# Two-head sweeps of an mLSTM encoder layer in a fixed order of steps

## The chip, the cores and the metric

The kernel runs on one core of a Trainium2 chip. The metric is the time of one execution on the device in microseconds (us). The core has five engines that each run a queue of their own: PE (matrix products), DVE (vector), ACT (scalar engine), POOL (GpSimd) and SP, which here only issues DMA transfers.

## The reference

One layer on two sequences, of 1024 and 256 rows with 1024 columns each, in float32. A conditioning vector gives a shift, a scale and a gate. The normalized rows go through one wide input projection, whose columns feed a gated convolution branch and a bidirectional mLSTM branch with four heads of width 256. Both branches are projected, merged with gates, projected once more and normalized:

```python
mod = c @ w_ada + b_ada
shift, scale, gate = split(mod, 3)
h = rms_norm(x, norm_g) * (1 + scale) + shift
cb, cc, cx, cz, q, k, v, o, mz, gpre, gmerge = split(h @ w_in)
y_conv = cb * dwconv3(cc * cx) * silu(cz)
hm = mlstm(q, k, v, i, f) + flip(mlstm(flip(q), flip(k), flip(v), ...))
y_m = sigmoid(o) * rms_norm_per_head(hm) * silu(mz)
merged = g_conv * (y_conv @ w_proj_conv) + g_mlstm * (y_m @ w_proj_mlstm)
out = rms_norm(x + gate * (merged @ w_out), final_norm_g)
```

The mLSTM runs in chunks of 128 rows, eight for the first sequence and two for the second, in each direction: a query against the state C, the chunk's own scores, and an update of C.

```python
S = (qc @ kc.T) * Dexp
num = S @ vc + inter_w * (qc @ C)
den = max(abs(sum(S) + inter_w * (qc @ n)), exp(-m_t))
h = num / den
C_new = decay * C + (w * kc).T @ vc
```

## The kernel before

A product of two float32 matrices is made as three products of rounded halves: a high part H, which ACT casts, and a low part L, which is the difference to it, taken by POOL or DVE. Four stages follow one another. First come the normalization and the shift and scale. Then comes the input projection in blocks of 1024 × 640, by Strassen's scheme (`run`); beside it, as generators that take one step per projection block, run the gate's part of the conditioning product (`thirds`) and the decay weights (`weights`). The third stage is the mLSTM with the convolution's projection as filler. The last stage merges, projects and normalizes.

Up to the end of the input projection the engines run their instructions in the order in which the program is written (a manual schedule, the context `hand`, closed before the third stage). From there on a scheduler of the language orders each engine's instructions by its own priorities and by when it expects them to be ready.

In the third stage a backward sweep of a head goes through its ten chunks and stores each query's result in `qcb`. A forward sweep goes the other way and makes the output. The sweep of a chunk consists of these parts, whose tiles the profile names:

- `prep`: ACT makes `vH`, DVE `vL`, the two parts of the weighted values; the parts `kH`, `kL` of the keys are loaded.
- `query`: ACT and POOL split the query into `qH` and `qL`; six products `pq` with the parts `CH`, `CL` of the state (`C0H`, `C0L` forward, `C1H`, `C1L` backward in the old kernel); ACT scales the result into `qcf` (forward) or `qcb` (backward).
- `state`: six products `pu`; DVE updates `C`; ACT casts its high part, POOL takes the low part.
- scores: products of `qT` and `kT`; DVE multiplies them with the decay weights `abc` and sums them into `den`; for two chunks at a time DVE makes `r`, the reciprocal of the denominator.
- tail: ACT and DVE form `Pt` from both directions, PE turns it, ACT copies it to `Ps`, PE multiplies it with the values, DVE adds the queries' results (`sums` below), and ACT sums the squares.
- output: the norm over the row's squares (six small operations of DVE and a root on ACT), ACT scales the rows, PE transposes them, DVE multiplies with the gate `og`, and a DMA stores to `ym_dr`.

The sums are written into the value tile `vN`, and the output is made for blocks of 640, 384 and 256 rows (`mlstm_out`). The filler `zc_units` makes 32 units of 24 products of 320 columns (`acc`), which a hand-written table FILL places among the steps of the forward sweeps. The backward sweep of the next head begins with step 5 of a forward sweep of 18 steps.

Of the kernel before, what the change touches and what calls it, by code (L numbers as in the profile page):

```python
# [41 lines left out]
def encoder_kernel(  # L42
# [776 lines left out]
    def thirds(pool):  # L819

        def total(acc, n):
            pg = misc_tile()
            PE.matmul(pg[0:1, 0:2 * P], ones[:, 0:1], acc[:].rearrange("p s n -> p (s n)"), start=True, stop=True)
            yield
            V.tensor_scalar(out=acc[0:1].rearrange("p s n -> p (s n)"), in0=pg[0:1, 0:2 * P], scalar1=0.5, scalar2=None,
                            op0=ALU.mult)
            for s in range(2):
                store(gb_dr[s:s + 1, n * P:(n + 1) * P], acc[0:1, s])

        late = iter(())  # L830
        for n in range(KT):
            ns = slice(2 * D + n * P, 2 * D + (n + 1) * P)
            acc = pool.tile([P, 2, P], F32, tag="acc", bufs=2, name="gacc")
            G.memset(acc[:], 0.0)
            for s in range(2):
                dma(acc[0:1, s], b_ada[0:1, ns])
            for k in range(0, KT, 4):
                raw = pool.tile([P, 4, P], F32, tag="wg", bufs=1, name="wg")
                dma(raw[:], wada[:, k:k + 4, ns])
                next(late, None)  # L840
                yield
                next(late, None)
                yield
                for i in range(4):
                    for s in range(2):
                        V.scalar_tensor_tensor(out=acc[:, s], in0=raw[:, i], scalar=cols[:, 8 * s + k + i:8 * s + k + i + 1],
                                               in1=acc[:, s], op0=ALU.mult, op1=ALU.add)
            late = chain([None], total(acc, n))
        for _ in late:
            yield  # L850
# [203 lines left out]
    hand.close()  # L1054

# [25 lines left out]
    for i in range(2):  # L1081
        G.memset(vNs[i][:, :, HD:HD + 1], 1.0)
        G.memset(vNs[i][:, :, HD + 1:HD + 2], 0.0)

# [3 lines left out]
    def load_head(h, what):  # L1088
        i, hs = h % 2, slice(h * HD, (h + 1) * HD)
        for t0, tn in ((640, 384), (0, 640), (1024, 256)):  # L1090
            ts_ = slice(t0, t0 + tn)
            cs = slice(t0 // P, (t0 + tn) // P)
            if "k" in what:
                dma(kTs[i][:, :, ts_], kT_dr[hs, ts_].rearrange("(b p) t -> p b t", p=P))
            if "v" in what:
                dma(vNs[i][:, cs, 0:HD], v_dr[ts_, hs].rearrange("(c p) d -> p c d", p=P))
            if "q" in what:
                dma(qTs[i][:, :, ts_], qT_dr[hs, ts_].rearrange("(b p) t -> p b t", p=P))

    vp = mstack.enter_context(tc.tile_pool(name="vp", bufs=2))  # L1100
    mp_ = mstack.enter_context(tc.tile_pool(name="ml", bufs=2))

    def split(pool, src, tag, shape, bufs=2, leng=V):
        H = pool.tile(shape, F32R, tag=tag + "H", bufs=bufs, name=tag + "H")
        L = pool.tile(shape, F32R, tag=tag + "L", bufs=bufs, name=tag + "L")
        A.copy(H[:], src)
        leng.tensor_tensor(out=L[:], in0=src, in1=fp(H[:]), op=ALU.subtract)  # L1107
        return H, L

    class Sweep:  # L1110


        def __init__(self, h, d):
            self.h, self.d = h, d
            self.kT, self.vN, self.qT = (x[h % 2] for x in (kTs, vNs, qTs))
            if d:
                self.todo = [c for c0, n in SEQS for c in range(c0 + n - 1, c0, -1)]
            else:
                self.todo = [c for c0, n in SEQS for c in range(c0, c0 + n - 1)]
            self.ahead = [self.prep(self.todo.pop(0))]  # L1120

        def prep(self, c):
            kH, kL = (mp_.tile([P, HD], F32R, tag="k" + part, bufs=4, name="k" + part) for part in "HL")
            for t, src in zip((kH, kL), kn_dr):
                dma(fp(t[:]), src[c * P:(c + 1) * P, self.h * HD:(self.h + 1) * HD])
            wcol = gcol[:, 3, self.d, self.h, c:c + 1]
            wvH, wvL = (mp_.tile([P, HD + 2], F32R, tag="v" + part, bufs=3, name="v" + part) for part in "HL")
            A.activation(wvH[:], self.vN[:, c, :], AF.Copy, bias=0.0, scale=wcol)
            V.scalar_tensor_tensor(out=wvL[:], in0=self.vN[:, c, :], scalar=wcol, in1=fp(wvH[:]), op0=ALU.mult,
                                   op1=ALU.subtract)  # L1130
            return kH, kL, wvH, wvL

        def query(self, c, dst):
            tsl = slice(c * P, (c + 1) * P)
            pq = psM.tile([P, 512], F32, tag="qc", bufs=1, name="pq")
            qH, qL = split(mp_, self.qT[:, :, tsl], "q", [P, 2, P], leng=G)
            CH, CL = self.parts
            for n, (q, C) in enumerate(((qH, CH), (qL, CH), (qH, CL))):
                for kd in range(2):
                    PE.matmul(pq[:, 0:HD + 2], q[:, kd, :], C[:, kd, :], start=n + kd == 0, stop=n + kd == 3)  # L1140
            A.activation(dst, pq[:, 0:HD + 2], AF.Copy, bias=0.0, scale=gcol[:, 1, self.d, self.h, c:c + 1])

        def state(self, c, first):
            kH, kL, wvH, wvL = self.ahead.pop(0)
            if self.todo:
                self.ahead.append(self.prep(self.todo.pop(0)))
            pu = psM.tile([P, 2, 512], F32, tag="u", bufs=1, name="pu")
# [5 lines left out]
            C = Cbuf[self.d]  # L1153
            if first:
# [4 lines left out]
            self.parts = split(mp_, C[:], f"C{self.d}", [P, 2, HD + 2], bufs=1, leng=G)  # L1159

    def backward(h):
        sw = Sweep(h, 1)
        for (c0, n) in SEQS:
            for c in range(c0 + n - 1, c0 - 1, -1):
                if c < c0 + n - 1:
                    sw.query(c, qcbs[h % 2][:, slot(c), :])
                if c > c0:
                    sw.state(c, c == c0 + n - 1)
                yield

    def forward(h):

        vN, kT, qT, qcb, ssqm = (x[h % 2] for x in (vNs, kTs, qTs, qcbs, ssqms))
        sw = Sweep(h, 0)

        def chunk_pair(c0, n, g):

            abc = abcs.pop(0)
            den = mp_.tile([P, 2, 2], F32, tag="den", name="den")
            r = mp_.tile([P, 2, 2], F32, tag="r", name="r")  # L1180
            qcf = mp_.tile([P, 2, HD + 2], F32, tag="qcf", name="qcf")
            for j in range(2):
                c = g + j
                tsl = slice(c * P, (c + 1) * P)
                if c > c0:
                    sw.query(c, qcf[:, j, :])
                if c < c0 + n - 1:
                    sw.state(c, c == c0)
                yield
                pS = misc_tile()  # L1190
                for kd in range(2):
                    PE.matmul(pS[:, 0:P], qT[:, kd, tsl], kT[:, kd, tsl], start=kd == 0, stop=kd == 1)
                inter = (qcf[:, j, HD:HD + 1] if c > c0 else 0.0,
                         qcb[:, slot(c), HD:HD + 1] if c < c0 + n - 1 else 0.0)
                for d in range(2):
                    V.tensor_tensor_reduce(out=abc[:, d, j, :], in0=pS[:, 0:P], in1=abc[:, d, j, :], op0=ALU.mult,
                                           op1=ALU.add, scale=KSC, scalar=inter[d], accum_out=den[:, j, d:d + 1])

            V.scalar_tensor_tensor(out=r[:], in0=den[:], scalar=-1.0, in1=gcol[:, 2, :, h, g:g + 2].rearrange("p d j -> p j d"),
                                   op0=ALU.mult, op1=ALU.max)  # L1200
            V.tensor_tensor(out=r[:], in0=r[:], in1=den[:], op=ALU.max)
            V.reciprocal(r[:], r[:])
            yield

            Ps = [None, None]

            def tail1(j):
                Pt = mp_.tile([P, P], F32, tag="Pt", name="Pt")
                A.activation(Pt[:], abc[:, 0, j, :], AF.Copy, bias=0.0, scale=r[:, j, 0:1])
                V.scalar_tensor_tensor(out=Pt[:], in0=abc[:, 1, j, :], scalar=r[:, j, 1:2], in1=Pt[:],  # L1210
# [21 lines left out]
            def both():  # L1232
                tail1(1)
                tail2(0)
# [102 lines left out]
    def drain(it):  # L1337
        for _ in it:
            pass
# [193 lines left out]
```

## Time and profile before

| | us |
|---|---|
| median of 3 runs | 1823.41 |
| lowest and highest run | 1821.04 and 1828.21 |
| profiled execution | 1823.46 |
| its span, first to last instruction | 1821.7 |

| engine | busy us | share of the span |
|---|---|---|
| PE | 1693.2 | 93% |
| DVE | 1030.8 | 57% |
| POOL | 831.4 | 46% |
| ACT | 667.6 | 37% |

A row of a view by groups gives the line, the engine, the operation, the tiles and shapes and the count, then the busy time in us and the mean of one in ns, then the engine's idle time just before and what ended it. A row of the waits gives who waited for whom, the total in us, the times and the longest. A row of the chain of waits or of the timeline starts with the start and the duration in us. Products are pipelined, so the pace of PE is the distance of their starts and not the duration of one.

### The profile page before, as it was taken

Reading aid. Unit: us, or ns where it says so; the run is one execution under the profiler, and the core shown is the slowest. Engines: PE = TensorE matmul, PEld = TensorE weight load, DVE = VectorE, ACT = ScalarE, POOL = GpSimd, SP = SyncE. Lnnn points to the kernel's source line nnn. Section 1 sums busy time; section 2 is a strip of 40 time slices with the busy share of each in tenths; the row PEclk is TensorE's granted clock in tenths of the full one; section 3 lists DMA queues with packets and bytes.
Section 4 is the critical chain, followed back from the end, with each engine's and each line's share of the span. In section 5 each row is a group of like instructions: output and inputs, shape, how many; then the busy total and the mean of one; then the engine's idle time right before and its main releaser. Section 6 shows DMA issues by size and latency. Waiting matters only on the chain.

```text
span 1821.7 us, 30022 instructions
## 1 busy us (share of the span) xinstructions
PE 1693.2 (93%) x11438; PEld 1630.9 (90%) x11438; DVE 1030.8 (57%) x1739; ACT 667.6 (37%) x1359; POOL 831.4 (46%) x661
## 2 busy tenths in 40 slices
PE   5789999999899999999999999996888788899997
PEld 1689999999788999999999999996877678799997
DVE  6874333277987554555555333332588777456645
ACT  6552333223434222222222223122576565434323
POOL 3443333234545466666665433333566364232422
PEclk9889999999999999999999999998999999999999
DMA  8223234223655222222221534349767865674631
GB/s 308 63 87 108 98 104 133 84 85 92 168 146 145 62 64 76 76 76 72 68 69 46 167 96 145 121 135 318 256 205 225 282 184 163 217 244 152 225 128 70
DMA packets 231427, 253.28 MB, mean 139 GB/s; under 512 B 13700, under 2 KB 190068, under 8 KB 230260
## 3 DMA queue, kind: packets, MB, share of 16 engines
q1 hardware_dynamic: 231284, 251.37, 43.7%
q8 instruction: 90, 1.47, 0.3%
q14 instruction: 53, 0.43, 0.1%
HBM read 177.85 MB, written 73.47 MB: 138 GB/s over the span
## 4 chain that ended last, share of the span: by engine, by line
PE 54%; DVE 6%; POOL 3%; issue 2%; DMA 2%; ACT 2%; SPq 0%; DVEq 0%; POOLq 0%; ACTq 0%
PE accx L337 35%; PE accd L1312 2%; PE accd L1313 2%; PE accd L1314 2%; PE accd L1423 2%; PE accd L1424 2%; PE accd L1422 2%; PE pq L1140 1%; POOL C1L L1107 1%; PE acc L1313 1%; PE acc L1312 1%; PE acc L1314 1%; POOL wl L161 1%; POOL C0L L1107 1%; PE misc L627 1%
## 5 line engine op out<-in xcount | busy, mean ns | idle before, releaser
L409 DVE TENSOR_TENSOR q<-accx,q 128x640 f32<-128x640 f32 x288 | 233.3, 820 | 420.2 <-PE accx L337 368.0
L161 POOL TENSOR_TENSOR wl<-comb,wh 128x512 fp32r<-128x512 f32 x176 | 236.3, 1344 | 488.3 <-ACT wh L160 403.3
L161 POOL TENSOR_TENSOR wl<-raw,wh 128x512 fp32r<-128x512 f32 x196 | 270.8, 1386 | 194.2 <-ACT wh L160 179.1
L337 PE MATMUL accx<-half,wh 128*128 128x320 f32 x1408 | 268.2, 313 | 5.4 <-ACT wh L160 5.4
L160 ACT CAST wh<-comb 128x512 fp32r<-128x512 f32 x176 | 108.6, 620 | 388.7 <-DVE comb L379 305.7
L337 PEld LDWEIGHTS accx<-half,wh 128*128 128x128 f32 x1408 | 223.5, 190 | 6.8 <-ACT wh L160 5.6
L160 ACT CAST wh<-raw 128x512 fp32r<-128x512 f32 (+1 forms) x212 | 136.2, 648 | 92.5 <-PE accd L1313 27.9
L337 PE MATMUL accx<-half,wl 128*128 128x320 f32 x704 | 162.2, 312 | 0.8 <-POOL wl L161 0.8
L498 ACT ACTIVATE q<-q,zero 128x640 f32<-128x640 f32 x80 | 66.4, 830 | 174.4 <-DVE q L409 155.3
L337 PEld LDWEIGHTS accx<-half,wl 128*128 128x128 f32 x704 | 119.0, 190 | 1.5 <-POOL wl L161 1.5
L1423 PE MATMUL accd<-wl,mH 128*128 128x256 f32 x320 | 90.2, 282 | 0.1
L1422 PE MATMUL accd<-wh,mH 128*128 128x256 f32 x320 | 90.1, 282 | 0.0
L1424 PE MATMUL accd<-wh,mL 128*128 128x256 f32 x320 | 90.0, 282 | 0.0
L337 PE MATMUL accx<-b10H,wh 128*128 128x320 f32 x352 | 82.4, 315 | 6.1 <-ACT q L934 5.9
L337 PE MATMUL accx<-t2H,wl 128*128 128x320 f32 x352 | 81.9, 314 | 4.2 <-POOL wl L161 4.1
L337 PE MATMUL accx<-b00H,wh 128*128 128x320 f32 x352 | 81.8, 314 | 2.4 <-DVE half L248 2.3
L337 PE MATMUL accx<-t2H,wh 128*128 128x320 f32 x352 | 82.4, 316 | 1.8 <-ACT wh L160 1.7
L1312 PE MATMUL acc<-y,wh 128*128 128x320 f32 x256 | 81.8, 323 | 0.7 <-ACT wh L160 0.3
L1313 PE MATMUL acc<-y,wh 128*128 128x320 f32 x256 | 81.2, 317 | 1.1 <-DMA y<-yc_drL 1.1
L337 PE MATMUL accx<-t3H,wh 128*128 128x320 f32 x352 | 80.6, 310 | 1.1 <-ACT wh L160 1.1
L1312 PE MATMUL accd<-y,wh 128*128 128x320 f32 x256 | 78.1, 313 | 3.5 <-DVE og L1283 3.5
L337 PE MATMUL accx<-b10H,wl 128*128 128x320 f32 x352 | 81.1, 312 | 0.2 <-POOL wl L161 0.2
(304 smaller groups left out, 4539.5 us busy)
## 6 DMA issues: line engine op xcount, KB each, us to landing
raw<-in_w_in_dram SPq DMA_DIRECT2D x96, 256.0 KB
raw<-in_w_in_dram SPq DMA_DIRECT2D x44, 512.0 KB
th_dr<-q SPq DMA_DIRECT2D x32, 320.0 KB
th<-th_dr SPq DMA_DIRECT2D x32, 320.0 KB
wa<-in_w_ada_dram SPq DMA_DIRECT2D x8, 1024.0 KB
raw<-in_w_proj_conv_dram SPq DMA_DIRECT2D x16, 512.0 KB
kH<-kn_drH SPq DMA_DIRECT2D x64, 128.0 KB
kL<-kn_drL SPq DMA_DIRECT2D x64, 128.0 KB
```

Source lines behind the costliest of these rows:

```text
L160: A.copy(wh[:], src)
L161: eng.tensor_tensor(out=wl[:], in0=src, in1=fp(wh[:]), op=ALU.subtract)
L337: PE.matmul(acc[:, q, 0:TQ], st_[:, k, :], m_[:, q * TQ:(q + 1) * TQ], start=k == 0 and n == 0, stop=k == 3 and n == 2)
L409: V.tensor_tensor(out=two(dst), in0=ps, in1=two(t), op=ALU.add)
L498: A.activation(out, in_, AF.Tanh, bias=zero[:, 0:1], scale=0.5)
L1107: leng.tensor_tensor(out=L[:], in0=src, in1=fp(H[:]), op=ALU.subtract)
L1312: PE.matmul(accs[q][:, :TQ], wh, yH, start=kt == 0, stop=False)
L1313: PE.matmul(accs[q][:, :TQ], wh, yL, start=False, stop=False)
L1314: PE.matmul(accs[q][:, :TQ], wl, yH, start=False, stop=kt == KT - 1)
L1422: PE.matmul(pd, sH, ws[0][:, k, :], start=kt == 0, stop=False)
L1423: PE.matmul(pd, sH, ws[1][:, k, :], start=False, stop=False)
L1424: PE.matmul(pd, sL, ws[0][:, k, :], start=False, stop=kt == KT - 1)
```

## The change

The manual schedule stays open through the third stage, so each engine runs the order in which that stage is now written. The stage becomes a loop of 56 steps. In step s the forward sweep handles one chunk (`F`), the backward sweep of the next head another (`B_`), the tail of the chunk before (`T1`) is merged and turned, and the one two before (`T2`) is multiplied with the values. Every second step makes the norm of the pair that began four steps earlier, and the two halves of its output stand in that step and in the next.

Steps 0 to 9 hold the first backward sweep with two halves of filler each, 10 to 49 the forward sweeps of the four heads, with a backward sweep in 11 to 40, and 50 to 55 the tails. A half is 12 of a unit's 24 products; the table HALVES says how many a step gets. The sums are written into `qcf` instead of the value tile, and the norm is made for two chunks at a time, 20 times in all instead of 12. Stores are issued at the start of the step after the one that makes them. In `thirds` the same operations are placed by a table of steps, the gate sum (`total`) one step later and its row another step later.

```diff
-    hand.close()
-
     sstack.close()
...
+        def keep_row(n):
+            V.tensor_scalar(out=accs[n][0:1].rearrange("p s n -> p (s n)"), in0=sums[n][0:1, 0:2 * P], scalar1=0.5,
+                            scalar2=None, op0=ALU.mult)
...
         for n in range(KT):
...
+            for t, order, f in ((0, 3, (begin, n)), (0, 2, (load, n, 0)), (1, 0, (bias, n)), (2, 0, (use, n, 0)),
+                                (2, 1, (load, n, 1)), (4, 0, (use, n, 1)), (6, 1, (total, n)), (7, 0, (keep_row, n))):
+                plan.setdefault(4 * n + t, []).append((order, f))
...
+        def sums(self, c):
+            g, j = c - c % 2, c % 2
+            first, last = self.ends(c)
+            r, hm, src = self.r[g], self.qcf[g][:, j, :HD], self.pv[:, :HD]
+            if not first:
+                V.scalar_tensor_tensor(out=hm, in0=hm, scalar=r[:, j, 0:1], in1=src, op0=ALU.mult, op1=ALU.add)
+                src = hm
...
+            A.activation(junk[:], hm, AF.Square, bias=zero[:, 0:1], scale=1.0, accum_out=ssqms[self.i][:, c:c + 1])
...
+        def norm(self, g):
+            sv, rv = ssqms[self.i][:, g:g + 2], rstms[self.i][:, g:g + 2]
+            V.tensor_scalar(out=sv, in0=sv, scalar1=1.0 / HD, scalar2=EPS, op0=ALU.mult, op1=ALU.add)
+            rsqrt_newton(mp_, rv, sv, 2)
             for j in range(2):
+                hm = self.qcf[g][:, j, :HD]
+                A.activation(hm, hm, AF.Copy, bias=0.0, scale=rv[:, j:j + 1])
...
+    HALVES = (2,) * 11 + (1, 0, 1, 1, 0, 1, 0, 1, 0) + (1, 1, 1, 1, 1, 0, 0, 0, 0, 1) + (1, 0, 1, 0, 1, 0, 1, 0, 1, 0) + (2,) * 16
+    END = FIRST + 10 * NH
+    for s in range(END + 6):
...
+        if F:
+            h, c = F
+            fw[h].query(c, pr[h].inter)
+            fw[h].state(c)
+            fw[h].carry(c)
+            pr[h].score(c)
+            pr[h].weigh(c)
+        nxt = at_bw.get(s + 1)
+        if HALVES[s] > 1 or (HALVES[s] and not B_):
+            fills.half()
+            fills.after()
+        if T2:
+            pr[T2[0]].values(T2[1])
+            pr[T2[0]].sums(T2[1])
+        nf = chunk_at(s + 1)
+        if nf:
+            fw[nf[0]].prep(nf[1])
+        if B_:
+            h, i = B_
+            bw[h].query(i, lambda c, h=h: qcbs[h % 2][:, slot(c), :])
+            bw[h].state(i)
+        if T1:
+            pr[T1[0]].merge(T1[1])
+        if B_:
+            bw[B_[0]].carry(B_[1])
+        if T1:
+            pr[T1[0]].turn(T1[1])
+        if HALVES[s]:
+            fills.half()
+            fills.after()
+        if nxt:
+            bw[nxt[0]].prep(nxt[1])
+        for lag, f in ((4, 0), (5, 1)):
+            G_ = chunk_at(s - lag)
+            if G_ and G_[1] % 2 == 0:
+                if f == 0:
+                    pr[G_[0]].norm(G_[1])
+                pr[G_[0]].result(G_[1], f)
...
+    hand.close()
+    ym0.append(load_y(ym_dr, 0))
     mstack.close()
     bstack.close()
```

What the change moves is seen best at three places in the middle of the third stage. The first is ACT's queue, between two results of a forward query (`qcf<-pq`). Before, in a forward sweep beside a backward one:

```order
L1141 ACTIVATE qcf<-pq,gcol 128x258
L1106 CAST qH<-qT_12157 128x256
L1215 COPY Ps<-misc 128x128
L1128 ACTIVATE vH<-vN_12156,gcol 128x258
L1106 CAST C0H<-C_12146 128x516
L1141 ACTIVATE qcb_12144<-pq,gcol 128x258
L1106 CAST qH<-qT_12154 128x256
L1128 ACTIVATE vH<-vN_12156,gcol 128x258
L1230 ACTIVATE qcf,ssqm_12149<-vN_12153,zero 128x256
L1106 CAST C1H<-C_12147 128x516
```

Now, one whole step with both sweeps (`C_12145` is the forward state, `C_12146` the backward one):

```order
L1158 ACTIVATE qcf<-pq,gcol 128x258
L1183 CAST CH<-C_12145 128x516
L1262 ACTIVATE junk,ssqm_12148<-qcf,zero 128x256
L1137 CAST qH<-qT_12153 128x256
L1143 ACTIVATE vH<-vN_12152,gcol 128x258
L1158 ACTIVATE qcb_12143<-pq,gcol 128x258
L1237 ACTIVATE Pt<-abc,r 128x128
L1183 CAST CH<-C_12146 128x516
L1245 COPY Ps<-misc 128x128
L1137 CAST qH<-qT_12156 128x256
L1143 ACTIVATE vH<-vN_12155,gcol 128x258
```

The squares (`junk,ssqm`) now stand ahead of both casts for the next forward chunk and of Pt, and the backward state's cast ahead of Ps and of both casts for the next backward chunk.

The second place is DVE's queue around a norm (`ssqm` to `rstm`). Before, in the norm of five chunks:

```order
L1270 TENSOR_SCALAR ssqm_12149<-ssqm_12149 128x5
L501 SCALAR_TENSOR_TENSOR th<-th,acc 128x320
L1129 SCALAR_TENSOR_TENSOR vL<-vN_12156,gcol,vH 128x258
L138 RECIPROCAL rs_r<-rs_r 128x5
L139 TENSOR_TENSOR rs_t<-rs_r 128x5
L140 TENSOR_TENSOR rs_t<-rs_t,ssqm_12149 128x5
L141 TENSOR_SCALAR rs_t<-rs_t 128x5
L1157 SCALAR_TENSOR_TENSOR C_12147<-C_12147,decay,pu 128x516
L142 TENSOR_TENSOR rstm_12151<-rs_t,rs_r 128x5
L1129 SCALAR_TENSOR_TENSOR vL<-vN_12156,gcol,vH 128x258
L1155 COPY C_12146<-pu 128x516
```

Now, from the second half of Pt to the result:

```order
L1238 SCALAR_TENSOR_TENSOR Pt<-abc,r,Pt 128x128
L1180 SCALAR_TENSOR_TENSOR C_12146<-C_12146,decay,pu 128x516
L1144 SCALAR_TENSOR_TENSOR vL<-vN_12155,gcol,vH 128x258
L1270 TENSOR_SCALAR ssqm_12148<-ssqm_12148 128x2
L138 RECIPROCAL rs_r<-rs_r 128x2
L139 TENSOR_TENSOR rs_t<-rs_r 128x2
L140 TENSOR_TENSOR rs_t<-rs_t,ssqm_12148 128x2
L141 TENSOR_SCALAR rs_t<-rs_t 128x2
L142 TENSOR_TENSOR rstm_12150<-rs_t,rs_r 128x2
L1281 SCALAR_TENSOR_TENSOR og<-misc,mhq,og 128x256
```

Other work that stood between the first operation and the reciprocal, and between the last two, has gone from there, and the result that needs the norm follows it at once.

The third place is PE's queue around the transposes for an output. Before:

```order
L1312 MATMUL acc<-y,wh 128x320
L1282 MATMUL misc<-ident,vN_12156 128x128
L1192 MATMUL misc<-kT_12152,qT_12154 128x128 x2
L1282 MATMUL misc<-ident,vN_12156 128x128 x3
L1150 MATMUL pu<-vH,kH 128x258
L1140 MATMUL pq<-C0H,qH 128x258 x2
L1140 MATMUL pq<-C0H,qL 128x258
```

Now, from the end of a half of the filler over the transposes (`ident,qcf`) to the next step's query and state:

```order
L1362 MATMUL acc<-y,wl 128x320
L1279 MATMUL misc<-ident,qcf 128x128 x2
L1157 MATMUL pq<-CH,qH 128x258 x2
L1157 MATMUL pq<-CH,qL 128x258 x2
L1157 MATMUL pq<-CL,qH 128x258 x2
L1168 MATMUL pu<-vH,kH 128x258
L1169 MATMUL pu<-vH,kL 128x258
L1170 MATMUL pu<-vL,kH 128x258
```

Single products of several units stood beside one another before; now each group is whole, and the next step's query and state follow the transposes.

More of the change, by code (lines that the diff above doesn't have):

```diff
@@ L831, in thirds @@
-        for n in range(KT):
[L832 to L848, printed above, removed]
@@ L849, in thirds, with begin, bias, load @@
-        for _ in late:
+        plan, accs, raws, sums = {}, {}, {}, {}
+        def begin(n):
+            accs[n] = pool.tile([P, 2, P], F32, tag="acc", bufs=2, name="gacc")
+            G.memset(accs[n][:], 0.0)
+        def bias(n):
+            for s in range(2):
+                dma(accs[n][0:1, s], b_ada[0:1, 2 * D + n * P:2 * D + (n + 1) * P])
+        def load(n, j):
+            raws[n] = pool.tile([P, 4, P], F32, tag="wg", bufs=1, name="wg")
+            dma(raws[n][:], wada[:, 4 * j:4 * j + 4, 2 * D + n * P:2 * D + (n + 1) * P])
@@ new lines, in use, with total @@
+        def use(n, j):
+            for i in range(4):
+                for s in range(2):
+                    k = 8 * s + 4 * j + i
+                    V.scalar_tensor_tensor(out=accs[n][:, s], in0=raws[n][:, i], scalar=cols[:, k:k + 1],
+                                           in1=accs[n][:, s], op0=ALU.mult, op1=ALU.add)
+        def total(n):
+            sums[n] = misc_tile()
+            PE.matmul(sums[n][0:1, 0:2 * P], ones[:, 0:1], accs[n][:].rearrange("p s n -> p (s n)"), start=True, stop=True)
@@ L850, in thirds @@
+        for t in range(max(plan) + 1):
+            for _, f in sorted(plan.get(t, ()), key=lambda x: x[0]):
+                f[0](*f[1:])
             yield
@@ L1114, in __init__ @@
             self.h, self.d = h, d
[L1115 to L1131, printed above, removed]
@@ L1133, in query @@
-        def query(self, c, dst):
-            tsl = slice(c * P, (c + 1) * P)
+            self.vN, self.qT = vNs[h % 2], qTs[h % 2]
+            self.order, self.first, self.has_state, self.has_query = [], set(), set(), set()
+            for c0, n in SEQS:
+                cs = list(range(c0, c0 + n))
+                if d:
+                    cs.reverse()
+                self.order += cs
+                self.has_state.update(cs[:-1])
+                self.has_query.update(cs[1:])
+                self.first.add(cs[0])
@@ L1378, in encoder_kernel, with chunk_at, plan @@
-    drain(fill)
-    drain(out)
+    FIRST = 10
+    fills = Filler()
+    fills.load_w(0)
+    load_v(0, 5, 8)
+    fw, bw, pr = {}, {}, {}
+    at_bw = {}
+    for h in range(NH):
+        bw[h], fw[h], pr[h] = Sweep(h, 1), Sweep(h, 0), Pairs(h)
+        for i in range(NC):
+            at_bw[10 * h + i + (h > 0)] = (h, i)
+    def chunk_at(s):
+        h, c = divmod(s - FIRST, NC)
+        return (h, c) if 0 <= h < NH else None
+    todo3 = {}
+    def plan(s, f, *args):
+        todo3.setdefault(s, []).append((f, args))
@@ new lines, in encoder_kernel @@
+    for h in range(NH):
+        s0 = FIRST + 10 * h
+        if h:
+            b0 = 10 * h + 1
+            free = FIRST + 10 * (h - 2)
+            for c0, c1, last in ((5, 8, 7), (0, 5, 4), (8, 10, 9)):
+                plan(max(2, free + last + 1), load_piece, h, c0, c1)
+                plan(max(2, free + last + 2), load_v, h, c0, c1)
+        else:
+            for c0, c1 in ((0, 5), (8, 10)):
+                plan(0, load_piece, h, c0, c1)
+                plan(0, load_v, h, c0, c1)
+        for g in range(0, NC, 2):
+            plan(s0 + g - 2, pr[h].load, g)
+            plan(s0 + g + 2, pr[h].load_og, g)
```

401 lines of the change are left out of this document (203 added, 198 removed).

## The prediction

> **What bounds the kernel now.** I read the busy time by stretches first. The change rewrites the stage between the last product of the input projection and the first product of the merge; its two stretches are 1244–1301 us (first backward sweep) and 1301–1582 us (four forward sweeps with the other backward sweeps among them).
>
> ```profile
> core 0: us, PE busy (x) PEld busy (x) DVE busy (x) ACT busy (x) POOL busy (x), PEclk, DMA share, GB/s
> 1244.00:1301.00 57.00, 49.67 (x319) 47.69 (x320) 16.85 (x30) 20.42 (x43) 26.94 (x24) 0.92 0.91 312
> 1301.00:1582.00 281.00, 237.74 (x1579) 212.94 (x1577) 212.57 (x556) 174.72 (x456) 148.27 (x135) 0.98 0.66 207
> ```
>
> PE is busy 85% of the second stretch, DVE 76%, ACT 62%: no engine is full, and each waits for the others. The stretch holds 40 forward chunks, so 281/40 = 7.0 us for each. The waits of the stage, and then of the projection stage, show where PE itself stands:
>
> ```profile
> PEld pq L1140 <- POOL C1L L1107: 17.9, 25, 2.0
> ...
> PE misc L1192 <- DMA qT<-qT_dr: 11.5, 1, 11.5
> ```
>
> ```profile
> PE misc L823 <- DVE gacc L846: 9.0, 7, 3.6
> ```
>
> The first is 25 short waits (0.7 us) for a state's low part, the second the stage's first load. The third is the gate sum in the projection stage. The chain of waits gives the pace of PE where it waits for nothing, and the merge's start:
>
> ```profile
> 1199.91 6.74 PE accx L337 x46
> ...
> 1267.70 0.73 PE pq L1140 x6
> 1269.25 0.76 DVE C L1157
> 1270.03 0.64 ACT C1H L1106
> ...
> 1582.32 0.63 PE accd L1312
> ```
>
> So 0.147 us for a filler product, 0.122 us for a sweep product. A half unit (12 products) is 1.76 us; a query and a state (12) are 1.46 us. From the end of a state on DVE to its cast on ACT go 0.02 us.
>
> **The change part by part.** *The gate sum.* Its product moves one step, so some 48 projection products (7.0 us), further behind its inputs. The longest of the seven waits was 3.6 us: all 9.0 us go. DVE has the same instructions; the two biases and the row's store move one step too, on SP, where nothing waits for them. I take −9 us, between −12 and 0 (0 if weights become late instead).
>
> *Steps 0 to 9, the first backward sweep.* Each step has two halves, a query and a state: 3.52 + 1.46 = 5.0 us on PE. The 5.2 MB of conv halves now stand ahead of the pieces of keys and queries on SP; at the 312 GB/s above they take 17 us, so the first steps run behind the loads. Ten steps end near 1304 us, within 1299 to 1312; before, the first forward query ran at 1301 (the second stretch is cut there), with 16 halves done where the new order has 20. This part costs 3 us.
>
> *Steps 10 to 49.* Here the whole sum lies. The engines run their rows in order, and the order rows show that in each two-head step ACT and DVE wait for each other twice. DVE: forward state, weights, sums; then ACT: squares, query cast, value cast, backward query's result, first half of Pt; then DVE: second half of Pt, backward state; then ACT: state cast, turned Pt, casts for the next backward step; then DVE: value rest, result, and only then the next forward state. The rows that price them (count and mean of the whole stage):
>
> ```profile
> L1129 DVE SCALAR_TENSOR_TENSOR vL<-vN,gcol,vH 128x258 fp32r<-128x258 f32 x64 | 44.2, 693 | 6.6 <-ACT vH L1128 6.6
> L1157 DVE SCALAR_TENSOR_TENSOR C<-C,decay,pu 128x516 f32<-128x516 f32 x48 | 35.8, 747 | 24.4 <-PE pu L1152 15.8 <-POOL C0L L1107 3.7 <-PE misc L1213 2.0
> L1210 DVE SCALAR_TENSOR_TENSOR Pt<-abc,r,Pt 128x128 f32<-128x128 f32 x40 | 19.4, 498 | 6.4 <-ACT Pt L1209 6.3
> L1228 DVE SCALAR_TENSOR_TENSOR vN<-qcb,r,vN 128x256 f32<-128x256 f32 x24 | 17.8, 744 | 0.4
> ...
> L1224 DVE SCALAR_TENSOR_TENSOR vN<-qcf,r,misc 128x256 f32<-128x256 f32 x32 | 15.3, 477 | 7.1 <-PE misc L1220 7.1
> L1196 DVE CUSTOM_DVE_ANT_0 abc<-misc,abc,qcf 128x128 f32<-128x128 f32 x32 | 11.1, 347 | 10.3 <-PE misc L1192 7.2 <-ACT qcf L1141 2.9
> L1196 DVE CUSTOM_DVE_ANT_0 abc<-misc,abc,qcb 128x128 f32<-128x128 f32 x32 | 11.0, 345 | 0.7 <-ACT qcb L1141 0.7
> L1155 DVE COPY C<-pu 128x516 f32<-128x516 f32 x16 | 10.9, 682 | 11.9 <-PE pu L1152 11.7
> L1199 DVE SCALAR_TENSOR_TENSOR r<-den,gcol 128x4 f32<-128x4 f32 x20 | 10.6, 528 | 0.1
> ...
> L1283 DVE SCALAR_TENSOR_TENSOR og<-misc,mhq,og 128x256 f32<-128x256 f32 x16 | 7.5, 479 | 5.6 <-DMA og<-og_dr 3.4 <-PE misc L1282 1.4 <-PE acc L1313 0.7
> L1201 DVE TENSOR_TENSOR r<-r,den 128x4 f32<-128x4 f32 x20 | 7.3, 365 | 0.1
> ...
> L1196 DVE CUSTOM_DVE_ANT_0 abc<-misc,abc 128x128 f32<-128x128 f32 x16 | 4.6, 286 | 3.3 <-PE misc L1192 3.3
> ...
> L1228 DVE SCALAR_TENSOR_TENSOR vN<-qcb,r,misc 128x256 f32<-128x256 f32 x8 | 3.8, 481 | 3.3 <-PE misc L1220 3.3
> ...
> L1202 DVE RECIPROCAL r<-r 128x4 f32<-128x4 f32 x20 | 3.4, 169 | 0.2
> ```
>
> ```profile
> L1128 ACT ACTIVATE vH<-vN,gcol 128x258 fp32r<-128x258 f32 x64 | 32.3, 510 | 26.4 <-PE pu L1151 19.7 <-DMA qT_dr<-q 4.7 <-DMA vN<-v_dr 1.5
> L1106 ACT CAST qH<-qT 128x256 fp32r<-128x256 f32 x64 | 25.5, 398 | 3.4 <-PE pq L1140 3.4
> L160 ACT CAST wh<-raw 128x512 fp32r<-128x512 f32 x37 | 22.6, 617 | 34.5 <-PE accd L1313 14.4 <-PE acc L1313 9.2 <-PE accx L337 5.8
> L1230 ACT ACTIVATE qcf<-vN,zero 128x256 f32<-128x256 f32 x40 | 20.3, 508 | 19.8 <-DVE vN L1228 17.7 <-DVE vN L1224 1.9
> L1106 ACT CAST C1H<-C 128x516 fp32r<-128x516 f32 x32 | 19.8, 618 | 4.0 <-DVE C L1157 2.8 <-DVE C L1155 1.1
> ...
> L1209 ACT ACTIVATE Pt<-abc,r 128x128 f32<-128x128 f32 x40 | 15.1, 395 | 8.4 <-DVE r L1202 8.0
> L1141 ACT ACTIVATE qcb<-pq,gcol 128x258 f32<-128x258 f32 x32 | 15.1, 472 | 27.5 <-PE pq L1140 27.4
> ...
> L1215 ACT COPY Ps<-misc 128x128 f32<-128x128 f32 x40 | 10.3, 259 | 10.5 <-PE misc L1213 10.3
> L1230 ACT ACTIVATION_READ_ACCUMULATOR qcf<-vN,zero 128x1 f32 x40 | 7.5, 187 | 0.0
> ```
>
> Forward share, four heads. On DVE: states 23.4 (half of 35.8 + 10.9), weights 26.7, r 21.3, sums 36.9, Pt 19.4, results 40 × 0.479 = 19.2, together 146.9 us. On ACT: squares 27.8, half of the query casts 12.8 and of the value casts 16.2, Pt 15.1, Ps 10.3, together 82.2. Backward share, the three heads whose sweep runs here: 0.75 × (states 23.3 + state casts 19.8 + query casts 12.7 + value casts 16.1 + value rests 22.1 + results 15.1) = 81.8. Two-product weight casts for ten splits: 20 × 0.617 = 12.3. The forward value rest, the forward state's cast and POOL's parts lie beside these.
>
> The norm is now made 20 times instead of 12 and stands at the end of every second step, with the transposes that need it in the same step, and PE's next query and state behind those. Its length stands undisturbed at the end of the stage, just after the last filler result:
>
> ```profile
> 1573.72 0.49 DVE L501 SCALAR_TENSOR_TENSOR th<-th,acc 128x320 f32<-128x320 f32 x1
> ...
> 1575.31 0.79 DVE L1270 TENSOR_SCALAR ssqm<-ssqm 128x2 f32<-128x2 f32 x1 [0.67 <-ACT qcf L1230]
> ...
> 1578.78 0.48 DVE L1283 SCALAR_TENSOR_TENSOR og<-misc,mhq,og 128x256 f32<-128x256 f32 x1 [1.36 <-PE misc L1282]
> ```
>
> From the norm's first instruction to the result it is 3.5 us; I take 3.2, as the first was itself long. 20 × 3.2 = 64. Behind it the forward state waits for PE's query and state: 20 × 1.46 = 29.2. In the last head, without a backward sweep, the second half stands between Pt and the next step: 10 × 1.76 + 5 × 1.46 = 24.9.
>
> All: 146.9 + 82.2 + 81.8 + 12.3 + 64 + 29.2 + 24.9 = 441 us. Of this goes what neighbours on one engine overlap:
>
> ```profile
> 1355.43 0.47 DVE L1283 SCALAR_TENSOR_TENSOR og<-misc,mhq,og 128x256 f32<-128x256 f32 x1
> 1355.83 0.34 DVE L1196 CUSTOM_DVE_ANT_0 abc<-misc,abc,qcf 128x128 f32<-128x128 f32 x1
> ```
>
> The second starts 0.07 us before the first ends. With 14 such neighbours in a two-head step and 10 in the others (counted in the order) and 0.08 each: 30 × 1.12 + 10 × 0.8 = 42. Five hand-overs a step of 0.05 (0.02 above; 0.05 as they cross PE too) give back 10. Left: 409 us, 10.2 a step.
>
> *Steps 50 to 52 and the hand-over.* A last chain with norm (9), then two steps of halves (5 and 3.5), and 9 us from the last filler result to the first merge product, as before (1573.7 to 1582.3): 27 us.
>
> The merge then starts at 1304 + 409 + 27 = 1740 instead of 1582: +158. With −9: +149. The profiled execution took 1823.46 us (span 1821.7), the median of the runs 1823.41: 1972, which I round to **1970 us**.
>
> *Bounds.* Low: many DVE means carry stalls, as this row shows (shortest, median, longest):
>
> ```profile
> L1129 DVE SCALAR_TENSOR_TENSOR vL<-vN,gcol,vH x64: 453/482/1601, 1238.6 to 1529.6; 128x258 fp32r<-128x258 f32 x64
> ```
>
> Of the mean of 693, 30% lies above the median. The same share of the r, second sums, Pt and value rests on the chain, 0.30 × (21.3 + 17.8 + 19.4 + 16.6) = 23, and a quarter of the norms, 16, make 39 us that go without stalls; twice the overlap takes 42 more: 1891. High: stalls twice as large (+39) and hand-overs of 0.1 us (+10): 2021.
>
> On these stalls the Trainium skill (SBUF — State Buffer, Who interferes with whom) says that of a DVE instruction with two SBUF inputs and a GpSimd one that reads SBUF, whichever starts second blocks until the first ends. The longest of 1601 ns, against 482, agrees. By that rule the fixed order would put r or the second sum under POOL's state rest in every step: nearer to the high bound.
>
> **The rivals.** *A: the orders overlap as written, and DVE's own work is the bound (faster).* Its 212.6 us and eight more norms of 3.2 us make 238; with 1304 and 27 the merge starts at 1569, 13 us earlier, and with −9 the time is about 1801. It decides if ACT finds squares, casts and Pt ready whenever DVE turns to something else. For it: DVE's 76%, and products a step behind. Against: on ACT the squares stand ahead of the casts and Pt that DVE needs next. The Trainium skill (Perfetto Trace Analysis, Optimization Strategy) advises working on the most contended engine, here PE, and feeding it earlier; by it the gaps of PE would fall, which is this side.
>
> *B: one of the two exchanges is hidden.* Without the second wait for ACT (0.618 + 0.259 + 0.398 + 0.510 = 1.8 us) a step takes 8.4 us: 336 instead of 409, so 1899. For it: 7.0 us now, with the same instructions. Against: the same ACT rows.
>
> *C: PE's clock falls as well.* In each step PE waits some 4 us for Pt and every second step 4 us for the norm. The first stretch above, which follows the wait of 11.5 us, has the clock at 0.92; the second, with short waits, 0.98. At half speed the 29 us of queries and states and 25 us of halves on the chain cost up to 54 more: 2024. The Trainium skill (TensorE: Matmul & The Clock Gate, Part 1) says that one idle window of about 3.4 us halves the clock. By that rule nearly every one of these waits could trip it; the rows above say only that long waits do.
>
> **How the numbers follow.** Forecast 0.60, B 0.15, C 0.12, A 0.11, and 0.02 that nothing measurable changes. The range of 1885 to 2035 takes in B, both bounds and C, and leaves out A. A difference of 0.5% (9 us) is about the least that a measurement of this kernel can tell from none. Faster 0.11, within 0.5% 0.02, slower 0.87.
>
> **What would show it.** Right: the stretch from the first forward query to the first merge product near 440 us, with PE, DVE and ACT all busy less than 60%; ACT's squares waiting for DVE, DVE's Pt for ACT, PE's transposes of Pt for DVE and of rows for ACT, each near 40 or 20 times; no wait of PE for the gate sum. Wrong: DVE or PE over 85% there, steps of 6 us (A), or long waits on loads, which I count as hidden.

## The result and the profile after

The changed kernel takes **2027.8 us** (median of 4 runs, 2025.8 to 2029.7) against 1822.2 us for the kernel before, run beside it: 1.112 times as long (95% interval 1.109 to 1.115), 205.6 us more. The profiled execution took 2027.5 us, its span 2025.7. The forecast of 1970 lay 58 us below, with the result in its range of 1885 to 2035.

The first view is again the busy time by stretches: the first backward sweep, and then everything from the first forward query's result (1314.0) to the first product of the merge (1783.3). PEclk is PE's granted clock, 1 being full.

```profile
core 0: us, PE busy (x) PEld busy (x) DVE busy (x) ACT busy (x) POOL busy (x), PEclk, DMA share, GB/s
1241.00:1314.00 73.00, 61.68 (x378) 58.01 (x378) 20.51 (x34) 21.88 (x47) 33.08 (x29) 0.89 0.86 293
1314.00:1783.00 469.00, 292.72 (x1520) 266.02 (x1518) 223.29 (x610) 178.59 (x463) 140.95 (x132) 0.80 0.38 120
```

The stage took 281 us before and takes 469 now. DVE's busy time has hardly changed (212.6 before, 223.3 now), nor ACT's (174.7 and 178.6). What was added is idle time on all engines: DVE is busy 48%, ACT 38%. PE is busy 62%, and more of it than before (237.7 to 292.7) although it runs fewer products (1579 to 1520): its granted clock fell from 0.98 to 0.80. The waits of this stretch say who waits for whom:

```profile
PE misc L1243 <- DVE Pt L1238: 111.2, 40, 4.5
...
PEld misc L1279 <- ACT qcf L1274: 71.7, 40, 5.4
DVE vL L1144 <- ACT vH L1143: 65.4, 44, 2.6
ACT junk L1262 <- DVE qcf L1259: 61.1, 32, 3.3
PE misc L1279 <- ACT qcf L1274: 60.8, 20, 5.1
DVE th L501 <- PE acc L1362: 55.8, 20, 3.7
...
DVE Pt L1238 <- ACT Pt L1237: 15.3, 13, 1.7
```

The same two waits of PE in the stage before (1301 to 1582):

```profile
PE misc L1282 <- ACT vN L1273: 10.0, 7, 3.9
...
PE misc L1213 <- DVE Pt L1210: 6.4, 8, 1.8
```

They go in a circle. ACT's squares wait for DVE's sums, DVE's value rests for ACT's casts, PE's transposes for Pt (40 times, 2.8 us each) and for the scaled rows (20 times, 3.0 us each). The row of `th` is one the prediction did not have: DVE waits for PE's filler product. The chain of waits over one step with a norm, from its sums to the next step's, shows the same circle in order of time (start, duration, what):

```profile
1482.79 0.41 DVE qcf L1256
1483.22 1.34 DVE qcf L1259
1484.64 0.60 ACT junk L1262 x2
1485.25 0.29 ACT qH L1137
1485.54 0.37 ACT qcb L1158
1485.91 0.30 ACT Pt L1237
...
1486.51 0.76 DVE C L1180
1487.29 0.62 ACT CH L1183
...
1489.56 0.61 DVE ssqm L1270
1490.20 0.30 ACT rs_r L137
...
1491.51 0.52 ACT qcf L1274
1492.07 0.88 PE misc L1279 x2
1492.95 1.29 PE pq L1157 x6
...
1496.83 0.50 DVE qcf L1259
```

Sums, squares, casts, Pt, state, state cast, norm, transposes, and only then the next forward query: each engine works while the others stand. The query's six products take 1.29 us here. At 0.122 us each, the pace before, they would take 0.73.

The whole chain of this stretch, by line and with its number of pieces:

```profile
by line: PE pq L1157 7.6%; issue 5.3%; PE acc L1360 5.2%; PE acc L1361 5.1%; PE acc L1362 5.1%; ACT junk L1262 4.9%; DVE qcf L1259 4.6%; PE misc L1214 4.1%; DVE vL L1144 4.0%; PE misc L1279 3.6%; DVE abc L1223 3.5%; DVE r L1230 3.1%; ACT vH
1929 pieces in order of time: start us, us, what
```

Added up over its pieces, PE holds 197 of the 469 us, DVE 153, ACT 83, hand-overs ("issue") 25, the rest 12. Filler alone (`acc`) is 15.4%, 72 us.

### The profile page after: what moved, and what is told of

Read it like the earlier page. It is cut to its first block, busy times and chain, and to the rows that moved or that the text cites. A ratio compares the mean times of both kernels' runs of the same rounds, so it can differ in the third digit from the quotient of the medians.

```text
span 2025.7 us, 30058 instructions
## 1 busy us (share of the span) xinstructions
PE 1755.5 (87%) x11438; PEld 1689.6 (83%) x11438; DVE 1034.1 (51%) x1795; ACT 672.1 (33%) x1367; POOL 829.4 (41%) x661
## 4 chain that ended last, share of the span: by engine, by line
PE 53%; DVE 9%; ACT 5%; DMA 3%; issue 3%; POOL 1%; SPq 0%; DVEq 0%; ACTq 0%; POOLq 0%
PE accx L337 31%; PE pq L1157 2%; PE accd L1539 2%; PE accd L1540 2%; PE accd L1538 2%; PE accd L1314 2%; PE accd L1312 2%; PE accd L1313 2%; PE acc L1360 1%; PE acc L1361 1%; PE acc L1362 1%; ACT junk L1262 1%; DVE qcf L1259 1%; PE misc L1214 1%; DVE vL L1144 1%
## 5 line engine op out<-in xcount | busy, mean ns | idle before, releaser
L1184 POOL TENSOR_TENSOR CL<-C,CH 128x516 fp32r<-128x516 f32 x64 | 83.1, 1299 | 273.9 <-ACT CH L1183 252.3
L1243 PE MATMUL misc<-ident,Pt 128*128 128x128 f32 x40 | 14.7, 366 | 111.2 <-DVE Pt L1238 111.2
L1360 PE MATMUL acc<-y,wh 128*128 128x320 f32 x256 | 97.3, 380 | 12.5 <-DMA y<-yc_drH 12.5
L1243 PEld LDWEIGHTS misc<-ident,Pt 128*128 128x128 f32 x40 | 6.1, 153 | 121.4 <-DVE Pt L1238 73.2
L1361 PE MATMUL acc<-y,wh 128*128 128x320 f32 x256 | 92.6, 362 | 3.3 <-DMA y<-yc_drL 3.3
L1362 PE MATMUL acc<-y,wl 128*128 128x320 f32 x256 | 91.7, 358 | 0.0
```

Source lines behind the costliest of these rows:

```text
L1184: G.tensor_tensor(out=CL[:], in0=C[:], in1=fp(CH[:]), op=ALU.subtract)
L1360: PE.matmul(self.acc[:, :TQ], wh, yH, start=kt == 0, stop=False)
L1361: PE.matmul(self.acc[:, :TQ], wh, yL, start=False, stop=False)
L1362: PE.matmul(self.acc[:, :TQ], wl, yH, start=False, stop=kt == KT - 1)
```

## The experiments

**The order alone.** Does the loss lie in the order or in the other edits?

```diff
+    hand.close()
     mp_ = mstack.enter_context(tc.tile_pool(name="ml", bufs=2))
...
-    hand.close()
     ym0.append(load_y(ym_dr, 0))
```

> Base is the changed kernel (2027.8 us); from the first backward sweep on, the order on the engines is left to the automatic scheduler, as it was before the change, with the changed kernel's operations (20 norms, sums in the query's tile, filler in half units, its loads). Theory 1 (the fixed order is what costs): the time falls most of the way back, to 1815 to 1870. Theory 2 (the other edits of the stage cost as much: more norms, the loads of the conv halves first, half units): above 1920.

Measured: 1819.6 us, 0.9987 of the kernel before (0.9973 to 1.0001). Theory 1 holds. In the stretch from the first forward query's result to the merge, nearly the same work (1516 products and 611 DVE instructions, against 1520 and 610) lies in 270 us:

```profile
1305.70:1575.40 269.70, 227.60 (x1516) 205.79 (x1514) 219.65 (x611) 173.76 (x461) 139.19 (x131) 0.97 0.66 209
```

So 20 norms, half units, sums in the query's tile and the new loads cost nothing that shows when the scheduler orders them. All of the 206 us is the fixed order, that of the loads on SP included; no run separates the engines' orders. This is also the fastest version tried; against the kernel before, the difference is at the edge of what the runs can tell.

**The gate sum alone**, in the kernel before: only the `thirds` part of the diff.

> Base is the kernel before (1823.4 us), with the gate sum's new order alone. By the prediction's term all of the 9.0 us of waits for the gate sum go: 1814. By the trace after the change, where the last projection product ends 3.7 us earlier and waits for low and high parts of weights grew by 5.6 us: 1819.5. Rival (something downstream waits anyway, for weights or the first query's load): within 1 us of 1823.

Measured: 1821.4 us, 0.9989 of before (0.9979 to 0.9999): a gain of 0.2 to 3.8 us, not 9. PE's other waits in that stretch (300 to 620 us) before, beside the 9.0 us for the gate sum, and then all its waits in this kernel:

```profile
PE accx L337 <- POOL wl L161: 3.9, 7, 0.9
PE accx L337 <- ACT wh L160: 2.5, 2, 1.4
```

```profile
PE accx L337 <- POOL wl L161: 7.8, 13, 0.9
PE accx L337 <- ACT wh L160: 4.4, 7, 1.2
PE accx L337 <- DVE q L409: 2.3, 1, 2.3
```

The wait for the gate sum is gone, and the waits for weights and for one accumulation took most of its place (6.4 to 14.5 us).

**The two waits, one at a time and together.** First, squares and forward casts go behind the turned Pt:

```diff
-        nf = chunk_at(s + 1)
-        if nf:
-            fw[nf[0]].prep(nf[1])
...
             pr[T1[0]].turn(T1[1])
+        if T2:
+            pr[T2[0]].square(T2[1])
+        nf = chunk_at(s + 1)
+        if nf:
+            fw[nf[0]].prep(nf[1])
```

> Base is the changed kernel (2027.8 us). In each step ScalarE's squares and its casts for the next forward step are issued behind the turned Pt instead of ahead of the first half of Pt; all the work is the same. Theory 1 (VectorE and ScalarE wait for each other in turn): the squares (0.51 + 0.19), the query cast (0.39) and the value cast (0.51) leave the path from the sums to Pt, 1.6 us in each of 40 steps, 64 us in all: about 1964, and the wait of PE for Pt (111 us) falls by some 60. Theory 2 (PE's clock and its waits for the norm set the step): Pt comes earlier, but the step stays, within 15 us of 2028. Theory 3 (ScalarE has no slack): the casts come too late for the next step and the time rises to 2040 or more.

Second, both results of a pair go to the end of the step after its norm:

```diff
-        for lag, f in ((4, 0), (5, 1)):
...
+        G_ = chunk_at(s - 5)
+        if G_ and G_[1] % 2 == 0:
+            for f in range(2):
+                pr[G_[0]].result(G_[1], f)
+        G_ = chunk_at(s - 4)
+        if G_ and G_[1] % 2 == 0:
+            pr[G_[0]].norm(G_[1])
```

> Base is the changed kernel (2027.8 us). The norm of a pair stays at the end of its step, and both of the pair's results (four transposes, two products on VectorE) move one step later, ahead of the next norm, so that no transpose stands behind the norm of its own step. Theory 1 (the norm stands in the chain as the prediction counted it: 20 x 3.2 us for itself and 20 x 1.46 for PE's query and state behind it): up to 93 us shorter, about 1935; PE's wait for the rows, 133 us on its two queues, is gone. Theory 2 (VectorE and ScalarE still need the norm's own time, and only PE is freed): the 29 us of query and state go and no more, about 1999. Theory 3 (the other exchange takes the whole step anyway): under 15 us.

And both:

> Base is the changed kernel (2027.8 us), with both edits together: squares and forward casts behind the turned Pt, results a step behind their norm. Theory 1 (one chain, each part of it a term of a sum): the two gains add, 64 + 93 = 157 us, about 1871. Theory 2 (the two waits lie in one another's shadow): the larger of the two gains alone, 1935 to 1960. If PE's granted clock also comes back to above 0.9 with the shorter waits, some 15 us more.

Measured: late squares 1992.7 us (−35), norm ahead 1986.9 (−41), both 1947.4 (−80). The gains add up, as for parts of one chain, but each is near half of its term in the sum (64 and 93). The 1947 lies in the range that theory 2 of the double edit named, but by its reason, with the gains as measured, only the larger one would be left: 1987. PE's waits for the norm's rows and for Pt in the kernel with late squares, and then for Pt in the one with the norm ahead (both in 1310 to 1740 us):

```profile
PE misc L1282 <- ACT qcf L1277: 71.4, 19, 6.0
...
PE misc L1243 <- DVE Pt L1238: 48.5, 39, 3.2
```

```profile
PE misc L1243 <- DVE Pt L1238: 130.2, 40, 6.1
```

With late squares PE's wait for Pt fell by 63 us, as theory 1 had it, while the time fell by 35, between theories 1 and 2. About 10 us were lost again at PE's next wait, for the norm's rows, which grew from 61 to 71 us, and POOL's share of the chain grew from 4 to 20 us; the rest is not split. With the norm ahead PE's wait for the rows is gone, and its wait for Pt grew from 111 to 130 us. Theory 2 there gave 1999; with the 29 us of query and state taken at the low clock (29 / 0.80 = 37), it comes to 1991, near the 1987 measured. The chain agrees with it: its pieces of the norm on DVE and ACT, from `ssqm` to the scaled rows, add up to 43 us in both kernels, while PE's queries, states and output transposes fall from 85 to 45 us.

**The half units.** Are they hidden?

```diff
-    HALVES = (2,) * 11 + (1, 0, 1, 1, 0, 1, 0, 1, 0) + ... + (2,) * 16
+    HALVES = (2,) * 11 + (0,) * 29 + (2,) * 21
```

> Base is the changed kernel (2027.8 us). The 16 half units of filler that stand in the two-head steps move behind the last step; the rest is as it was. At the end they run back to back, 16 x 1.76 = 28 us. Theory 1 (a half unit in a two-head step stands on the path, since the next query and state queue behind it on PE, at about 3 us): -16 x 3 + 28, about 2008. Theory 2 (a half unit there lies in PE's waits, as the prediction had it): +28, about 2056.

Measured: 2042.3 us (+14), between the two theories. Of the 28 us that the 16 halves take at the end, the two-head steps gave back 14: there a half unit costs about 0.9 us on the path, neither 0 nor 3. The four runs lie between 2036 and 2045 us, which makes it 0.7 to 1.2. Nor is it the price of the half alone: without the filler the granted clock of 1314 to 1735 us fell from 0.79 to 0.76.

**The clock.** The extra products fill PE's waits; they write parts of PE's result tiles that nobody reads (`spin`, given a tile and how many):

```diff
             pT = misc_tile()
+            fills.spin(pT, 12)
...
             py = misc_tile()
+            if db == 0:
+                fills.spin(py, 24)
```

> Base is the changed kernel (2027.8 us), with extra products that nobody reads, put on PE where it waits: 12 of 128x256 ahead of each transpose of Pt, and 24 ahead of the first transpose behind each norm; at 0.12 us they take 1.4 and 2.9 us, within the waits there (2.8 and 5 us). Theory 1 (the waits lower PE's clock, and slowed products lie on the path: 16 half units of 3.1 instead of 1.8 us and the queries and states behind them): the granted clock in the stage rises from 0.79 to 0.9 or more and the time falls by 20 to 50 us, to 1980 to 2008. Theory 2 (the slow products lie in PE's own slack): the clock rises and the time stays within 10 us of 2028. Theory 3 (the waits are no cause of the clock): the clock stays below 0.85 and the time rises by up to 60.

Measured: 1997.8 us, 30 us **faster** with some 940 products more. Theory 1 holds. The stretch from the first forward query's result to the merge:

```profile
1312.50:1757.20 444.70, 351.28 (x2457) 330.69 (x2455) 225.51 (x610) 178.55 (x463) 141.89 (x132) 0.93 0.40 128
```

The clock rises from 0.80 to 0.93 and the stretch shrinks from 469 to 445 us. PE's share of the chain falls from 197 to 150 us, although 17 us of it are now extra products; DVE's and ACT's stay (153 and 85).

The same filling with both edits in place:

> Base is the kernel with both early edits (late squares, norm ahead; 1947.4 us, granted clock 0.86 in the stage). Added are 12 unread products of 128x256 ahead of each transpose of Pt. Theory 1 (the clock costs in proportion to what PE has on the path): clock above 0.93 and 10 to 20 us less, 1928 to 1937. Theory 2 (with shorter waits the slowed products lie in slack): within 5 us of 1947, or slower by the products that no longer fit in the waits.

Measured: 1937.8 us, 9.6 us less, at the edge of theory 1. The clock went from 0.85 to 0.92 between first forward query and merge, where shorter waits had already brought back a part of it.

**Another fixed order.** Each engine's row gets first what is ready when the step begins. The loop is now, in short:

```diff
+        result(s - 5); merge(T2)
+        fw.query; fw.state; fw.carry
+        turn(T2); half
+        bw.query; bw.state; score(F); bw.carry; weigh(F)
+        values(T2); sums(T2); fw.prep; bw.prep; square(T2)
+        half; norm(s - 4)
```

> Base is the changed kernel (2027.8 us), with another fixed order of the same work: Pt, its transpose and the values of a chunk two steps behind its scores, the products of both heads and the scores ahead of them on PE, squares and casts last on ScalarE, the results of a pair at the start of the step after its norm. Theory 1 (an exchange costs only if what is asked for is not yet there): no transpose waits for Pt or for the norm, a step takes about 7.5 to 8 us, the clock comes back above 0.9: 1860 to 1900. Theory 2 (the state's own loop through PE, VectorE, ScalarE and GpSimd and back holds a step at 9 us or more): above 1930.

Measured: 1951.4 us (−76), clock 0.82; in theory 2's range, but its reason is not all: the results at the start of a step put PE's wait for the norm's rows in front of the next query (waits in 1310 to 1740 us):

```profile
PE misc L1282 <- ACT qcf L1277: 68.7, 20, 5.8
```

So the results went to the end of the step, and then also the norm to the middle:

> Base is the other fixed order (1951.4 us), in which PE still waited 69 us for the norm, since the results stood at the very start of the step behind it. Here the results stand at that step's end. Theory 1 (that wait is a part of the path): 40 to 70 us less, 1880 to 1910. Theory 2 (the norm's work on VectorE and ScalarE sets the step, not PE behind it): within 15 us of 1951.

> Base is the other fixed order (1951.4 us). Here the norm itself also moves, from the end of a step to the middle of the next (behind the scores' weights on VectorE), with its results at that step's end. Theory 1 (a wait is hidden as soon as products stand in its queue's way): VectorE and ScalarE meet in the norm while PE runs sums, values and a half unit: no worse than the kernel with only the results late, 1870 to 1910. Theory 2 (every meeting of VectorE and ScalarE in one step costs its full length wherever it stands): 10 to 30 us slower than that kernel.

Measured: 1927.5 us (−24, about half of what theory 1 gave and more than theory 2), then 1905.8 us (−22 more, theory 1). The last lies clearly below the 1930 to which theory 2 had the state's own loop hold this order. The latter's stretch:

```profile
1312.60:1661.80 349.20, 256.57 (x1520) 231.81 (x1519) 222.67 (x610) 176.42 (x463) 143.03 (x132) 0.88 0.50 162
```

This is the best fixed order tried: 122 of the 206 us come back, by moving nothing but places in the program. It is still 4.5% slower than the kernel before (1.0454, 1.0438 to 1.0470).

## Why the prediction was right, and what it mis-sized

*The mechanism.* The forecast was a chain in which DVE and ACT wait for each other twice a step and PE waits for Pt and for the norm. The trace has it: squares wait 40 times for the sums (32 + 8), the transposes of Pt 40 times, those of rows 20 times, and the runs show that two of its parts add up (−35, −41, both −80). Two of its signs came otherwise. DVE waited for ACT's half of Pt only 13 times; mostly it waited for ACT just before, at the forward value rest (`vL`: 44 waits with the backward ones, 65 us), which the sum had put beside the chain. And PE was busy 62%, not under 60%. Rival A did not come: the order does not overlap as written. Rival B neither: both exchanges are there.

*The gate sum.* −9 us was forecast. The last projection product ended 3.7 us earlier in the profile of the changed kernel, and alone the edit is worth 0.2 to 3.8 us. The step that failed is "all 9.0 us go"; the lower bound that the prediction named, weights that become late instead, is what mostly happened. That is 5 us of the miss.

*Steps 0 to 9.* 3 us were forecast; the first forward query's result is ready at 1314.0, and with the 3.7 us at 1317.7 in the old count, not 1304. The loads take longer than the 17 us assumed. The chain goes through them from 1239 to 1268:

```profile
1238.99 13.73 DMA y<-yc_drL
1252.73 8.88 DMA vN<-v_dr
1261.67 6.71 DMA raw<-in_w_proj_conv_dram
```

That is 14 us of the miss. The loads are not all of it: with the same operations ordered by the scheduler, the loads' issue too, that result was ready at 1305.7, so about 8 of the 14 go with the fixed order of these steps.

*Steps 10 to 52.* 409 + 27 = 436 us were forecast, and it took 469. The total is 33 us too low, but its parts are further off, in both directions. DVE and ACT were put on the path for 345 us of the 409 (the five terms without 29.2 and 24.9, less the overlap); the chain has them for 236. The forecast gave PE 54 and most of the 27, about 80; the chain has it for 197. The two errors, 109 us too much and 117 too little, nearly cancel, and that the total came within 33 us is luck to that extent. So the step that failed is the assumption that whatever DVE and ACT have to do in turn is never shorter than what PE does beside it. When they were done, it was often PE that was not, at its lower clock and with filler in its queue. That a term of 64 us, taken away, gave back only 35 fits this; of the 93 only 41 came back, since the norm's own work stayed on the chain.

*Rival C* was given 0.12 as a case by itself. It came together with the forecast: the clock fell to 0.80, and its 2024 us lies 4 us from the measured time. That nearness is luck in part, since keeping PE busy gives back 25 us of the stretch and 30 us of the time (the profiled execution was the slowest of the four) and not the 54 of this rival. What it priced at half speed was right in kind:

```profile
1372.70 0.28 PE L1168 MATMUL pu<-vH,kH 128*128 128x258 f32 x1
1372.82 0.28 PE L1169 MATMUL pu<-vH,kL 128*128 128x258 f32 x1
...
1373.29 0.28 PE L1170 MATMUL pu<-vL,kH 128*128 128x258 f32 x1
1375.37 0.33 PE L1243 MATMUL misc<-ident,Pt 128*128 128x128 f32 x1 [1.80 <-DVE Pt L1238]
...
1375.69 0.33 PE L1361 MATMUL acc<-y,wh 128*128 128x320 f32 x1
1375.83 0.45 PE L1362 MATMUL acc<-y,wl 128*128 128x320 f32 x1
1376.08 0.47 PE L1360 MATMUL acc<-y,wh 128*128 128x320 f32 x1
1376.34 0.47 PE L1361 MATMUL acc<-y,wh 128*128 128x320 f32 x1
```

This is PE's timeline: the end of a state, the wait for Pt, and the first products of a half unit. Starts lie 0.12 us apart in the state and 0.14 in the half, until 1376; after that 0.265. A half at that pace takes 3.2 us and not the 1.76 of the sum.

*The stalls of DVE under POOL* are there: the second sum took 1.34 us at 1483.22, beside a POOL instruction, and 0.50 at 1496.83, with none beside it, in the chain above. POOL's row in the timeline:

```profile
1482.98 1.29 POOL L1184 TENSOR_TENSOR CL<-C,CH 128x516 fp32r<-128x516 f32 x1 [1.41 <-ACT CH L1183]
```

The `r` group cost 29 us against 21 in the sum. With DVE's whole busy time 10.7 us longer than before, they explain little; no run took them away by themselves.

*The sum of the miss:* 5 (gate sum) + 14 (steps 0 to 9) + 33 (chain) + 3 (merge to the end, 242.4 against 239.4) + 2 (rounding 1972 to 1970) = 57, for 58 measured. The 33 are shown to hang on the clock for about 25; the rest is not split further.

## What to carry to other kernels

A fixed order is a program for five queues at once: a step is as long as its longest round trip unless each queue's next instruction is already ready, so look in the order for an instruction that waits and ask what stands behind it. When the chain of engine A and engine B is summed, sum also what the third engine does beside them, at the clock that it will have after waiting. And a term of such a sum is no forecast of what its removal gives: the two removals tried here were worth about half.

## What was not expected of the hardware

PE's clock fell after a wait well under 3 us. In the timeline above the pace is full up to 1373.3; PE then waits 1.80 us for Pt, starts again at the full pace, and 0.6 us later the pace halves. PE's busy time and the granted clock (0.50, 1.00, 0.50 and 1.00) of four stretches show what lies around it:

```profile
1369.10:1372.40 3.30, 3.30 (x15) 3.11 (x15) 2.75 (x9) 0.92 (x2) 1.76 (x3) 0.50 0.12 40
1372.50:1375.80 3.30, 1.50 (x12) 1.30 (x12) 1.61 (x3) 1.56 (x5) 1.23 (x2) 1.00 0.29 82
1375.90:1379.20 3.30, 2.78 (x11) 2.38 (x9) 0.57 (x3) 1.50 (x4) 2.00 (x2) 0.50 0.78 247
1379.30:1382.60 3.30, 0.93 (x6) 0.75 (x7) 1.44 (x8) 1.20 (x3) 0.00 (x0) 1.00 0.30 103
```

A stretch in which PE was mostly busy is followed by the full clock, one in which it was mostly idle by half. In this trace the recorded clock changes only at the edges of stretches of 3.41 us. From 1314 to 1783 us, 81 of these have the full clock: where PE was busy less than 45% of one, the next was always at half, and where more than 55%, always at full.

The Trainium skill (TensorE: Matmul & The Clock Gate, Part 1) gives one idle window of about 3.4 us as the cause of the lower rate. No wait of that length lies between the full pace and the half one here, so the measurement differs from it.

And work that does nothing paid: some 940 products that nobody reads made the kernel 30 us faster.
